# Layer 0 attention on Trainium2: scores in 64-row tiles with two heads side by side, linear attention in pieces at fixed places

## The chip, the core and the metric

The kernel runs on one core of one Trainium2 chip. A core has five engines with an instruction queue each: TensorE (PE in the profile, its weight loads PEld) multiplies matrices from SBUF into the accumulator memory PSUM, VectorE (DVE), ScalarE (ACT) and GpSimd (POOL) work element by element, and SyncE (SP) issues most DMAs. Each queue runs in its own order; an instruction that waits holds up all that stand behind it in the queue. The metric is the device time of one execution in microseconds, lower is better, shown as the median of several runs. The profile is one execution, with its span from the first to the last instruction.

## The reference

The model has two layers. Layer 0 runs two branches beside each other over 2304 tokens (256 context, 2048 latent); what is changed lies in these two, between their projections and the layer's output projection.

```python
def block_attention(q, k, v, scale):            # branch A: 8 heads of 64 + 32 = 96 dimensions
    ...
        s = jnp.einsum('bqhd,bkhd->bhqk', qi, k, preferred_element_type=jnp.float32) * scale
        p = jax.nn.softmax(s, axis=-1).astype(v.dtype)
        return jnp.einsum('bhqk,bkhd->bqhd', p, v)
...
def gla_scan(q, k, v, g, s0):                   # branch B: 4 heads, forward and backward, chunks of 64
    ...
    def step(state, inp):
        qi, ki, vi, gi = inp
        b = jnp.cumsum(gi, axis=-2)
        b_last = b[..., -1:, :]
        q_t = qi * jnp.exp(b)
        k_t = ki * jnp.exp(-b)
        att = jnp.where(mask, jnp.einsum('bhld,bhmd->bhlm', q_t, k_t), 0.0)
        o = jnp.einsum('bhld,bhde->bhle', q_t, state) + jnp.einsum('bhlm,bhme->bhle', att, vi)
        k_dec = ki * jnp.exp(b_last - b)
        state = state * jnp.exp(b_last)[..., 0, :, None] + jnp.einsum('bhld,bhle->bhde', k_dec, vi)
        return state, o
```

Of the 96 dimensions of a query and a key 64 are plain (`A_NOPE`) and 32 carry the rotary position (`A_ROPE`); a value has 64. Context queries attend to the 256 context keys, latent queries to all 2304. The gate logits of branch B come from 2 x 16 columns of the projection (`g_lr`); its result is normalised per head and gated before the output projection.

## The kernel before

**Attention (`even_attention`).** Everything is transposed: scores stand as [128 keys x up to 512 queries]. The outer loop goes over four head pairs `j`, the next over five query blocks (one of 256 context queries, four of 512 latent ones), the inner over key tiles of 128 keys: 18, or 2 for the context. For precision each operand of a score is split into two fp32r parts, high and low; of the four products three are taken: `kh` x `qh` (with a 97th row that carries a bias, L1097), `kh` x `ql` (L1098) and `kl` x `qh` (L1099), each over 96 or 97 rows of the array and 512 columns. They add up in one of three PSUM banks named `st`. ScalarE takes the exponential into SBUF (`apt`, L106, the helper through which all of ScalarE's operations go) and VectorE adds it to the running sum over keys (`acc`, L1088), head by head. Where six key tiles are pending, the value products of the four oldest are issued (`tail`, L1039): plain fp32, 64 columns of the array for each of the two heads, adding up in a bank `av`. `finish` then divides: two matmuls with a constant sum `acc` over keys (L970), and ScalarE's logarithm and exponential and VectorE's L975 to L977 make the quotient; it reads `av` directly, of which there are two banks.

**Linear attention (`gla`).** It goes over 18 chunks of 128 tokens in a first, a scanning and a second pass. `front` turns the gate columns round (L797), makes the logits (L803), the log-sigmoid (`ge`, `gG`) and its cumulated sums (L818, L819) and the factors `gqt`, `gkt`. `back` multiplies these with the inputs, turns them round (L847), makes the chunk's own state `D` (L852), the products within the chunk in 64-row tiles, backward and forward alternating (L861), and their output `goi` (L870). `scan` passes the states on: forward on GpSimd, backward on VectorE. `second` then adds the states' part (`enter`, L927 and L928), takes the sum of squares on VectorE, and in `leave` scales, gates and turns round (L945). All of it shares two PSUM banks `gl`.

**What sets the order.** The kernel is written against a framework that places each engine's instructions by its own estimate of when their inputs are ready; `issue_after` ties an instruction behind another one on its queue. Scores and value products are tied to each other, the pieces of the linear attention are not: the framework lays them between the score matmuls wherever they become ready. From key tile 174 on, `hook` gives out the second pass step by step (`next(slow)`), with the loads of the output projection's weights.

**Loads.** For each head pair, keys and their low parts come in thirds of 768 keys, one DMA for each, and queries in two DMAs per block, all issued by SyncE.

## Time and profile before

| | |
|---|---|
| median of 3 runs | 3543.79 us (3543.53 to 3548.53) |
| the profiled execution itself, its span | 3541.8 us |
| attention stretch of layer 0 | 1060 to 1902 us of the span |
| TensorE busy, whole span | 3477.8 us (98%) |
| VectorE, ScalarE, GpSimd busy, whole span | 2392.1, 1398.4, 1214.3 us |

The profiled execution lies 2.0 us below the median of the runs. In the groups of instructions, a row gives line, engine, operation, the tiles out<-in by the program's names, the shape and the count, then the busy time, the mean duration of one in ns, and the idle time of the engine ahead of them with what ended it. TensorE's instructions overlap, so their durations add up to more than the time they take. A plain fp32 matmul appears as two instructions and more on TensorE; the counts in the profile are of such instructions, those of the printed orders below of the program's.

### The profile page before, as it was taken

How to read it: one execution, taken by the hardware profiler on the slowest of the kernel's cores; microseconds unless marked ns; L12 is line 12 of the kernel's file. 1: busy time of each engine (PE TensorE's matmuls, PEld its weight loads, DVE VectorE, ACT ScalarE, POOL GpSimd, SP SyncE). 2: the span in 40 equal slices, each digit the busy share in tenths (PEclk: the TensorE clock that was granted, in tenths of full speed). 3: DMA queues.
4: the chain of work that ended last, by engine and by line, in shares of the span. 5: the costliest groups of instructions: out<-in, count | busy, mean ns of one | idle time of the engine just before them, and what ended most of it. 6: DMA issues, size and time to landing. Idle time of an engine off the chain costs nothing. (4 is left out here: it accounts for less than half of the span.)

```text
span 3541.8 us, 53493 instructions
## 1 busy us (share of the span) xinstructions
PE 3477.8 (98%) x19260; PEld 2752.4 (78%) x19260; DVE 2392.1 (68%) x5020; ACT 1398.4 (39%) x2656; POOL 1214.3 (34%) x1363
## 2 busy tenths in 40 slices
PE   8999999999999999999999999999999999999999
PEld 6998999999996666656667888888898987555587
DVE  4677767888886777788765345455598883777821
ACT  5555451111116555555553134444422223555510
POOL 1433330111111222211321233333354544777743
PEclk9999999999999999999999999999999999999999
DMA  6555564222243343434543554555844348878664
GB/s 246 161 148 169 149 196 116 78 76 85 68 124 83 80 111 85 101 84 115 161 119 126 169 174 124 143 161 156 255 152 146 123 128 224 217 210 218 187 184 149
DMA packets 386914, 513.75 MB, mean 145 GB/s; under 512 B 61229, under 2 KB 264061, under 8 KB 380746
## 3 DMA queue, kind: packets, MB, share of 16 engines
...
## 5 line engine op out<-in xcount | busy, mean ns | idle before, releaser
L1088 DVE TENSOR_TENSOR acc<-acc,apt 128x512 f32<-128x512 f32 x512 | 379.6, 772 | 142.2 <-ACT apt L106 139.5
L739 DVE TENSOR_REDUCE mm<-mx 128x1 f32<-128x512 f32 (+1 forms) x656 | 390.8, 628 | 87.8 <-PE mx L738 80.4
L106 ACT ACTIVATE apt<-st 128x512 f32<-128x512 f32 (+1 forms) x592 | 344.8, 594 | 247.3 <-PE st L1099 207.5
L1039 PE MATMUL av<-apt,av 128*64 128x512 f32 (+1 forms) x1184 | 270.0, 592 | 0.0
L1097 PE MATMUL st<-aq,akh 97*128 97x512 f32 x576 | 245.1, 426 | 1.0 <-ACT apt L106 1.0
L738 PE MATMUL mx<-mk,mq 96*128 96x512 f32 (+1 forms) x656 | 241.7, 371 | 0.0
L106 ACT ACTIVATE u<-gm 128x352 f32<-128x352 f32 (+1 forms) x144 | 70.8, 493 | 418.4 <-PE gm L131 182.6
L1098 PE MATMUL st<-aq,akh 96*128 96x512 f32 x576 | 228.2, 396 | 0.0
L1099 PE MATMUL st<-aq,akl 96*128 96x512 f32 x576 | 227.9, 396 | 0.0
L106 ACT ACTIVATE opt<-opt 128x930 f32<-128x930 f32 (+9 forms) x144 | 119.5, 831 | 254.5 <-POOL opt L1856 140.0
L1039 PEld LDWEIGHTS av<-apt,av 128*64 128x64 f32 x1184 | 80.1, 136 | 152.7 <-issue 149.7
L1554 DVE CUSTOM_DVE_ANT_1 mx<-mx,mtab 128x465 f32<-128x465 f32 (+12 forms) x576 | 180.3, 341 | 26.5 <-PE mx L1548 20.4
L1689 POOL TENSOR_TENSOR oacc<-oacc,opt 128x682 f32<-128x682 f32 (+9 forms) x144 | 170.3, 1200 | 40.6 <-ACT opt L106 39.1
L1818 DVE TENSOR_TENSOR opt<-st,tab 128x64 f32<-128x64 f32 (+10 forms) x576 | 142.3, 312 | 37.8 <-PE st L1654 33.2
L1097 PEld LDWEIGHTS st<-aq,akh 97*128 97x128 f32 x576 | 108.3, 188 | 72.6 <-issue 44.6
L1099 PEld LDWEIGHTS st<-aq,akl 96*128 96x128 f32 x576 | 109.5, 190 | 25.2
L738 PEld LDWEIGHTS mx<-mk,mq 96*128 96x128 f32 x656 | 123.3, 188 | 6.0
L1098 PEld LDWEIGHTS st<-aq,akh 96*128 96x128 f32 x576 | 109.9, 191 | 17.0
L106 ACT ACTIVATE x<-px,modB,modA 128x128 f32<-128x128 f32 x272 | 98.7, 465 | 55.9 <-PE px L362 32.5
L129 PE MATMUL gm<-w1h,hhi 128*128 128x512 f32 x288 | 115.1, 400 | 0.0
L1653 PE MATMUL st<-q,kt 128*128 128x480 f32 (+5 forms) x256 | 98.4, 386 | 16.8 <-DVE opt L1818 13.1
L131 PE MATMUL gm<-w0h,hlo 128*128 128x512 f32 x288 | 113.3, 393 | 1.5 <-DVE hlo L392 1.5
...
## 6 DMA issues: line engine op xcount, KB each, us to landing
...
```

Of the source, the lines that this page charges most:

```text
L106: return self.nc.scalar.activation(out, in_, func, **kw)
L129: self.nc.tensor.matmul(out, lh(k), rh(k), start=j == 0, stop=False)
L738: mm = nc.tensor.matmul(ps[:, :w], q[:A_QK, (t % 6) * P : (t % 6) * P + P], k[:A_QK, k0 : k0 + w], start=True, stop=True)
L739: nc.vector.tensor_reduce(out=m[:, t, n : n + 1], in_=ps[:, :w], axis=AX.X, op=ALU.max)
L1039: nc.tensor.matmul(O[j, nb][i * 64 : i * 64 + 64, :w], V[j, kt // TT][:, kt % TT, i * 64 : i * 64 + 64], pts[i][:, :w], start=n == 0, stop ...
L1088: self.add = nc.vector.tensor_tensor(out=acc[i][:, :w], in0=a[:, :w], in1=pts[i][:, :w], op=ALU.add)
L1097: nc.tensor.matmul(ps[:, :w], kh[: A_QK + 1, i, kq], qh[: A_QK + 1, :w], start=True, stop=False)
L1098: nc.tensor.matmul(ps[:, :w], kh[:A_QK, i, kq], ql[:A_QK, :w], start=False, stop=False)
L1099: mm = nc.tensor.matmul(ps[:, :w], kl[:A_QK, i, kq], qh[:A_QK, :w], start=False, stop=True)
L1554: nc.vector.tensor_tensor_reduce(out=s, in0=s, in1=tb[:, ri : ri + rn, ci : ci + cn], scale=1.0, scalar=-3e38, op0=ALU.add, op1=ALU.max, a ...
L1689: self.psum = nc.gpsimd.tensor_tensor(out=a, in0=a, in1=pts[:, :, a0 - r0 : a1 - r0, :], op=ALU.add)
L1818: badd = nc.vector.tensor_tensor(out=pt[:, d[0], d[1]], in0=ps[:, d[0], d[1]], in1=tabs[j][i][:, ri : ri + rn, ci : ci + cn], op=ALU.add)
```

## The change

**Scores.** `score` replaces the three products of each head by five of at most 64 rows: plain part high x high, high x low, low x high, then the rotary part's high and low keys (32 rows each, stacked) x high, and high x low with the bias row (33 rows). Head 0 of the pair lies on rows 0 to 63 of the array, head 1 on rows 64 to 127; the ten matmuls of a key tile alternate between them and are tied one behind the other. Keys, low parts and queries are laid out for it in SBUF: six DMAs for a third of the keys where there was one, two for the low parts, ten for a block of queries where there were two.

```diff
+        def score(j, kt, Q, ps, w):
+
+            kq = slice(kt % TT * P, kt % TT * P + P)
+            kh, kl = K[j, kt // TT], L[j, kt // TT]
+            mm = last_pe[0]
+            for k, kz, qz, n in ((kl, 0, 0, 64), (kl, 0, 1, 64), (kl, 1, 0, 64), (kh, 0, 2, 64), (kh, 1, 3, A_ROPE + 1)):
+                for i in range(2):
+                    r = slice(i * 64, i * 64 + n)
+                    with after(mm):
+                        mm = nc.tensor.matmul(ps[i], k[r, kz, kq], Q[r, qz, :w], start=qz == kz == 0 and k is kl, stop=k is kh and kz == 1)
+            last_pe[0] = mm
+            return mm
...
-                        ps = self.tl(pp, [P, 512], "st", bufs=3)
-                        nc.tensor.matmul(ps[:, :w], kh[: A_QK + 1, i, kq], qh[: A_QK + 1, :w], start=True, stop=False)
-                        nc.tensor.matmul(ps[:, :w], kh[:A_QK, i, kq], ql[:A_QK, :w], start=False, stop=False)
-                        mm = nc.tensor.matmul(ps[:, :w], kl[:A_QK, i, kq], qh[:A_QK, :w], start=False, stop=True)
-                        pt = self.tl(ap, [P, 512], "apt", bufs=14)
-                        ex = self.act(pt[:, :w], ps[:, :w], AF.Exp, scale=A_SCALE)
-                        pts.append(pt)
-                    add(n, pts)
+                    ps = [self.tl(pp, [P, 512], "st", bufs=4)[:, :w] for _ in range(2)]
+                    mm = score(j, kt, Q, ps, w)
+                    pt = self.tl(ap, [P, 2, 512], "apt", bufs=6)
                     for i in range(2):
+                        ex = self.act(pt[:, i, :w], ps[i], AF.Exp, scale=A_SCALE)
+                    if n == 0:
+                        first = pt
+                    else:
+                        self.add = nc.vector.tensor_tensor(out=acc[:, :, :w], in0=(first if n == 1 else acc)[:, :, :w], in1=pt[:, :, :w], op=ALU.add)
...
             for a, b in parts(j, p):
-                nc.sync.dma_start(kh[:A_QK, :, a:b].bitcast(F32),
-                                  self.KT[2 * j : 2 * j + 2, 0, :A_QK, p * W + a : p * W + b].rearrange("h p t -> p h t"))
+                for i in range(2):
+                    r, src = i * 64, self.KT[2 * j + i, :, A_NOPE:A_QK, p * W + a : p * W + b]
+                    for u, z in ((0, 0), (0, 1), (1, 0)):
+                        nc.sync.dma_start(kh[r + z * A_ROPE : r + z * A_ROPE + A_ROPE, u, a:b].bitcast(F32), src[z])
```

On TensorE one key tile of 512 queries reads as follows; `st` are the score banks, `aq` the queries, `akh` and `akl` the keys' tiles. Before:

```order
L1097 MATMUL st_12898<-aq_12816,akh_1772_10749 128x512
L1098 MATMUL st_12898<-aq_12816,akh_1772_10749 128x512
L1099 MATMUL st_12898<-aq_12816,akl_10761 128x512
L1097 MATMUL st_12904<-aq_12816,akh_1772_10749 128x512
L1098 MATMUL st_12904<-aq_12816,akh_1772_10749 128x512
L1099 MATMUL st_12904<-aq_12816,akl_10761 128x512
```

and with the change:

```order
L1216 MATMUL st_11689<-aq_11367,akl_10809 128x512
L1216 MATMUL st_11690<-aq_11367,akl_10809 128x512
L1216 MATMUL st_11689<-aq_11367,akl_10809 128x512
L1216 MATMUL st_11690<-aq_11367,akl_10809 128x512
L1216 MATMUL st_11689<-aq_11367,akl_10809 128x512
L1216 MATMUL st_11690<-aq_11367,akl_10809 128x512
L1216 MATMUL st_11689<-aq_11367,akh_1773_10750 128x512
L1216 MATMUL st_11690<-aq_11367,akh_1773_10750 128x512
L1216 MATMUL st_11689<-aq_11367,akh_1773_10750 128x512
L1216 MATMUL st_11690<-aq_11367,akh_1773_10750 128x512
```

Six steps, one head after the other, became ten, of which each two neighbours belong to different heads; the first bank is complete with the ninth instead of the third.

**PSUM, sums and the quotient.** There are four `st` banks, so that two key tiles of two heads fit, three `gl` banks, and one `av` bank; the bank `den` goes. VectorE adds both heads of a key tile in one instruction, 1024 wide. Where a block's value products end, ScalarE copies `av` to SBUF (`take`); the matmuls with the constant follow ahead of the next group of value products (`divide`), and VectorE's part (`newton`) behind that group's last key tile.

```diff
+        def flush():
+
+            dens, room = list(taken), 3 - len(taken)
+            taken.clear()
+            for x in dens:
+                run(ending, *x)
+            for x in [pend.pop(0) for _ in range(min(4, len(pend)))]:
+                if x[2] == 0 and taken and room:
+                    hook(room, run)
+                    room = 0
+                run(tail, *x)
+            if room:
+                hook(room, run)
...
+                    behind(ex, *([self.add] if n else []))
+                    if len(pend) == 6:
+                        flush()
+                    elif len(pend) == 4:
+                        hook(0, run)
```

**Linear attention.** `front` and `back` are cut into pieces, each with one TensorE part: `ranks` (three chunks at once, L812), `logits` (L823), `middle` (L842, L843), `turn` (L871), `local` (L881), `within` (L894), `inner` (L909); the second pass into `join` (L997) and `leave` (L1022). `run` ties each behind TensorE's last matmul, so that none stands between the scores of a key tile. A planner gives them out: behind each group of four value products as many as there are free `gl` banks (three), each piece only if what it reads was made a group earlier (`fwd`, `may`); halfway through the next four key tiles `hook(0)` issues the elementwise multiplications that `turn` reads (`times`) and one `within`. After the forward pass `enter` places one `leave` and one `join` behind each group; halfway run `scale` and `more`, which loads the output projection's weights one by one.

```diff
+        def may(what, c):
+
+            t = now[0]
+            if what == ranks:
+                return c % 3 == 0 and had(logits, c - 4)
+            return {logits: lambda: had(ranks, c - c % 3, t) and had(middle, c - 1),
+                    middle: lambda: had(logits, c, t) and had(turn, c - 1) and had(local, c - 1) and had(inner, c - 2),
+                    turn: lambda: had(middle, c, t) and had(within, c - 1),
+                    local: lambda: had(middle, c, t),
+                    within: lambda: had(turn, c) and had(inner, c - 1),
+                    inner: lambda: had(within, c, t) and had(local, c)}[what]()
...
+            for what in (inner, turn, local, middle, logits, ranks):
+                for c in range(NT):
+                    n = 2 if what == turn else 1
+                    if (what, c) not in done and n <= room and may(what, c):
+                        room -= n
+                        done[what, c] = now[0]
+                        picked.append((order.index(what), what, c))
```

Value products and what follows them read on TensorE as follows; `av` is their bank, `gl` a bank of the linear attention. Before:

```order
L1039 MATMUL av_12926<-apt_12874,av_10763 64x512
L1039 MATMUL av_12926<-apt_12880,av_10763 64x512
L1097 MATMUL st_12935<-aq_12816,akh_1773_10750 128x512
L1098 MATMUL st_12935<-aq_12816,akh_1773_10750 128x512
L1099 MATMUL st_12935<-aq_12816,akl_10772 128x512
L818 MATMUL gl_10917<-gG_10880,trr_10789 128x4x64
L819 MATMUL gl_10917<-ge_10882,trr_10789 128x4x64
L818 MATMUL gl_10917<-gG_10880,trr_10789 128x4x64
L819 MATMUL gl_10917<-ge_10882,trr_10789 128x4x64
L861 MATMUL gl_10932<-gqT_10890,gkT_10891 128x128
```

and with the change:

```order
L1166 MATMUL av_11543<-apt_11579,av_10812 64x512 x2
L1166 MATMUL av_11543<-apt_11600,av_10812 64x512 x2
L881 MATMUL gl_11659<-gu_10892,gkt_11432 128x128 x4
L842 MATMUL gl_11665<-gG_11447,trr_10833 128x4x64
L843 MATMUL gl_11665<-ge_11440,trr_10833 128x4x64
L842 MATMUL gl_11665<-gG_11447,trr_10833 128x4x64
L843 MATMUL gl_11665<-ge_11440,trr_10833 128x4x64
L823 MATMUL gl_11677<-gw_10827,rT_1792_10841 128x512
L1216 MATMUL st_11689<-aq_11367,akl_10809 128x512
```

The linear attention moved from between the scores to one place behind the value products, here with three pieces (`local`, `middle`, `logits`).

**Which engine does what.** The backward scan goes from VectorE to GpSimd, the copy of `D` and the sums of squares from VectorE to ScalarE:

```diff
-            nc.vector.tensor_copy(Dl[c][:].rearrange("p h t -> p (h t)"), ps[:])
+            self.act(Dl[c][:].rearrange("p h t -> p (h t)"), ps[:])
...
-        scan(list(range(NT)), slice(0, 64), nc.gpsimd, "gsf")
-        scan(self.back_order(), slice(64, 128), nc.vector, "gsb")
...
+                g.tensor_tensor(out=N[sl], in0=S[sl], in1=f[sl, 3, :].unsqueeze(2).to_broadcast([64, H, P]), op=ALU.mult)
+                g.tensor_tensor(out=N[sl], in0=N[sl], in1=d[sl], op=ALU.add)
+                g.tensor_tensor(out=d[sl], in0=S[sl], in1=f[sl, 1, :].unsqueeze(2).to_broadcast([64, H, P]), op=ALU.mult)
...
-                nc.vector.tensor_tensor_reduce(out=sq[:, o], in0=oi[:, o], in1=oi[:, o], scale=1.0, scalar=0.0,
-                                               op0=ALU.mult, op1=ALU.add, accum_out=ss[:, h : h + 1])
+                self.act(sq[:, each[h]], oi[:, each[h]], AF.Square, accum_out=ss[:, h : h + 1])
```

ScalarE's queue at the burst of scores that follows the rows above; every row is the helper L106, `apt` out of `st` is an exponential of scores. Before, around a comparable chunk:

```order
L106 ACTIVATE ge_11030<-gl_11028 128x512
L106 ACTIVATE apt_13138<-st_13134 128x512
L106 ACTIVATE ge_11030<-ge_11030 128x512
L106 ACTIVATE apt_13144<-st_13140 128x512
L106 ACTIVATE ge_11030<-ge_11030 128x512
L106 ACTIVATE apt_13150<-st_13146 128x512
L106 ACTIVATE goi_11045<-gl_11040 128x512
```

and with the change:

```order
L106 ACTIVATE D_1796_10851<-gl_11659 128x512
L106 ACTIVATE gqt_11670<-gl_11665 128x512
L106 ACTIVATE gkt_11671<-gl_11665 128x512
L106 ACTIVATE gt_11680<-gl_11677 128x512
L106 ACTIVATE gt_11680<-gt_11680 128x512
L106 ACTIVATE apt_11701<-st_11689 128x512
L106 ACTIVATE gt_11680<-gt_11680 128x512
L106 ACTIVATE apt_11701<-st_11690 128x512
L106 ACTIVATE apt_11717<-st_11705 128x512
L106 ACTIVATE apt_11717<-st_11706 128x512
L106 ACTIVATE gG_11686<-gt_11680 128x512
```

Where one instruction of the linear attention stood between two exponentials, five now stand ahead of the burst's first exponential and one between its two.

393 lines of the change are left out of this document (231 added, 162 removed).

## The prediction

> **What bounds the kernel now.** I read the page's first and fifth part, then layer 0's attention alone in the windows view, then what TensorE waits for there, then its timeline for the cadence. Ahead of the change's stretch and behind it nothing is edited, so those parts of the span are kept as they are.
>
> ```profile
> span 3541.8 us, 53493 instructions
> ...
> PE 3477.8 (98%) x19260; PEld 2752.4 (78%) x19260; DVE 2392.1 (68%) x5020; ACT 1398.4 (39%) x2656; POOL 1214.3 (34%) x1363
> ...
> L1097 PE MATMUL st<-aq,akh 97*128 97x512 f32 x576 | 245.1, 426 | 1.0 <-ACT apt L106 1.0
> ```
> ```profile
> 1060.00:1902.00 842.00, 836.17 (x4119) 521.39 (x4120) 628.13 (x1027) 482.03 (x926) 185.26 (x187) 1.00 0.38 101
> ```
> ```profile
> PE st L1097 <- ACT apt L106: 2.2, 3, 1.2
> PE gl L870 <- DVE gat L866: 1.8, 5, 0.6
> PE den L970 <- DVE rc L976: 1.4, 1, 1.4
> PE gl L803 <- DVE ge L864: 0.2, 1, 0.2
> ```
> The second fence is the attention stretch, 1060 to 1902 (behind the length: busy us and count of PE, PEld, DVE, ACT, POOL; granted clock; DMA share; GB/s), the third all waits of TensorE in it. The stretch is TensorE's: busy 836 of 842 us at the full granted clock (1.00), with only 5.6 us of waits, while VectorE (628), ScalarE (482) and GpSimd (185) have room. So a shorter instruction list on TensorE shortens the kernel, until another engine ends the wait. What one step costs there stands in the timeline:
>
> ```profile
> 1116.01 1.05 PE L852 MATMUL gl<-gu,gkt 128*128 128x128 f32 x8
> 1116.89 0.27 PE L797 MATMUL gl<-ident,gu 128*96 128x128 f32 x1
> ...
> 1118.18 0.40 PE L1099 MATMUL st<-aq,akl 96*128 96x512 f32 x1
> 1118.51 1.08 PE L970 MATMUL den<-acc,mtwos 128*64 128x512 f32 x4
> 1119.41 3.60 PE L1039 MATMUL av<-apt,av 128*64 128x512 f32 x16
> 1122.95 0.50 PE L1097 MATMUL st<-aq,akh 97*128 97x512 f32 x1
> 1123.29 0.40 PE L1098 MATMUL st<-aq,akh 96*128 96x512 f32 x1
> ...
> 1125.08 0.40 PE L1098 MATMUL st<-aq,akh 96*128 96x512 f32 x1
> ...
> 1126.72 0.40 PE L1099 MATMUL st<-aq,akl 96*128 96x512 f32 x1
> 1127.05 1.16 PE L861 MATMUL gl<-gqT,gkT 64*128 64x128 f32 x14
> 1128.13 0.50 PE L1097 MATMUL st<-aq,akh 97*128 97x512 f32 x1
> ```
> Durations overlap here, so I go by starts. Seven score steps lie between 1125.08 and 1126.72: 0.234 us each.
>
> **The scores: the gain.** Before, a key tile takes 2 heads x 3 products = 6 steps, 1.405 us; there are 576/2 = 288 such pairs 512 wide and 8 pairs 256 wide. After, it takes 10 matmuls of 64 rows, the two heads alternating on rows 0 to 63 and 64 to 127. If the two run side by side that is 5 steps, 1.17 us, and the gain is 288 x 0.234 + 8 x 0.12 = 68.4 us. Whether they do: L861 of the linear attention is already such an alternation. Its 14 instructions take 1128.13 - 1127.05 = 1.08 us; less 0.2 us for changing the array's form (below), that is 0.126 per pair, while one full-height L852 of the same width takes (1116.89 - 1116.01)/8 = 0.110. Two for the price of nearly one. But L861 is plain fp32, and the trace has no fp32r instruction of 64 rows. Bounds: quickest, a step costs what one pass of the value products does (16 instructions in 3.44 us without the form change, two heads side by side, two passes each: 0.215), which gives 288 x 5 x 0.019 = 27 us more; slowest, no overlap, 10 x 0.234 = 2.34 us, a loss of 269 us. I take 0.234: the tile's shape is L861's, the operand's rate is L1098's.
>
> The Trainium skill (TensorE: Matmul & The Clock Gate, Measured speedup vs the span model) lets packed tiles take one matmul's duration plus about 4 ns for each further tile. By it each step would be 4 ns dearer, an estimate of 288 x 5 x 0.004 = 5.8 us, and the sum below would end 6 us higher; no row here settles so small a term.
>
> **The fixed order: form changes.** Entering another form (full height, half height, half width) costs 1118.51 - 1118.18 - 0.234 = 0.10 us, and the first matmul in it lasts 1123.29 - 1122.95 = 0.34 instead of 0.234, another 0.11. Counted along TensorE's order between the first score and the last value product, there are 222 changes before and 221 after: scores now always differ in form from what surrounds them, but the linear attention no longer stands among them except for `within`, which has their form. I cost it at nothing. Its matmuls are as many as before (18 chunks of each piece).
>
> **Waits that go.** The pieces that waited for VectorE (L870, L970, L803: 3.4 us) now stand one group behind what they read: -3.4 us. Of L1097's 2.2 us, the longest (1.2) is at the first exponential; I leave all of it.
>
> **Waits that come: ScalarE.** Before, three score banks went round one by one, an exponential every 0.70 us of TensorE time, and linear-attention work was spread between them. After, the four banks are two pairs, and ScalarE's queue holds a whole group's linear-attention instructions ahead of the first exponential of the next four key tiles.
>
> ```profile
> 1414.22 1.30 ACT L106 ACTIVATE apt<-st 128x512 f32<-128x512 f32 x2
> ...
> 1414.49 0.40 PE L1099 MATMUL st<-aq,akl 96*128 96x512 f32 x1
> ```
> ```profile
> 1102.51 0.60 ACT L106 ACTIVATE gqt<-gl 128x512 f32<-128x512 f32 x1
> 1102.99 0.62 ACT L106 ACTIVATE gkt<-gl 128x512 f32<-128x512 f32 x1
> 1103.46 0.65 ACT L106 ACTIVATE ge<-ge 128x512 f32<-128x512 f32 x1
> 1103.98 1.60 ACT L106 ACTIVATE apt<-st 128x512 f32<-128x512 f32 x3
> ```
> ```profile
> 1103.93 0.40 PE L1099 MATMUL st<-aq,akl 96*128 96x512 f32 x1
> 1104.66 0.50 PE L1097 MATMUL st<-aq,akh 97*128 97x512 f32 x1 [0.34 <-ACT apt L106]
> ```
> An exponential starts 0.43 us behind its tile's last step (1414.22 + 1.30 - 0.60 = 1414.92, against 1414.49). Back to back, ScalarE starts one each 0.48 us (0.52 where it reads SBUF); one lasts 0.60, and TensorE follows 0.05 later. The last fence is the mechanism at work already: `gqt`, `gkt` and `ge` of the linear attention stood ahead of the exponentials, and TensorE came 0.50 us late (0.73 between the starts instead of 0.234).
>
> The walk of one burst of four key tiles, from its first step: pair 1's last step starts at 1.04, its exponentials run 1.47 to 2.07 and 1.95 to 2.55, and pair 3, due at 2.44, needs the second bank: **0.17 us late**, then the two heads run staggered and lose no more. Behind the waiting matmul stand, in TensorE's fixed order, the rest of the burst and the value products, so each such wait is lost in full. Where five instructions stand ahead (`local`, `middle`, `logits`: the first begins 0.6 before the burst, as its product is done) and a sixth between the two exponentials, the second exponential ends at 3.44: **1.05 late**. With `middle` or `logits` beside another piece, four to five ahead: **0.6**. In the second pass:
>
> ```profile
> L106 ACT ACTIVATE gsb<-gl,gn 128x128 f32<-128x128 f32 x72 | 20.4, 373 | 1.9 <-PE gl L945 1.8
> ...
> L106 ACT ACTIVATION_READ_ACCUMULATOR sql<-u 128x1 f32 x72 | 13.7, 190 | 0.0
> ...
> L928 DVE TENSOR_TENSOR goi<-gl,goi 128x512 f32<-128x512 f32 x18 | 12.4, 691 | 1.7 <-PE gl L927 1.5
> ```
> `join`'s four squares, moved from VectorE, wait for the 0.69 us add, start at about 0.9, and cost between 20.4/72 = 0.28 each and 0.28 + 0.19; I take 0.33, nearer the first, since neighbours overlap. The second exponential then ends at 3.3: **0.9 late**. By the printed order there are 8 bursts of the heavy kind, 10 of the middling, 17 with `join`, 18 that `within` cuts in two (its 1 us gives ScalarE time: 0), and 21 others: 8 x 1.05 + 10 x 0.6 + 17 x 0.9 + 21 x 0.17 = 33 us. From below, 56 x 0.17 = 9.5; from above, 1.1 in all 74, 81 us.
>
> **What I cost at nothing, and its cover.** GpSimd gets the backward scan:
>
> ```profile
> L907 POOL TENSOR_TENSOR gsf<-gsf,D 64x512 f32<-64x512 f32 x17 | 27.1, 1593 | 1.3
> L222 POOL TENSOR_TENSOR gss<-gss,mhalf 128x4 f32<-128x4 f32 x18 | 23.1, 1285 | 1.5
> L942 POOL TENSOR_TENSOR goi<-goi,gsf 128x512 f32<-128x512 f32 x18 | 22.9, 1272 | 34.6 <-issue 25.7 <-DVE goi L941 5.6 <-PE av L1039 1.7
> L908 POOL TENSOR_TENSOR D<-gsf,fac 64x512 f32<-64x512 f32 x17 | 22.7, 1335 | 1.3
> L906 POOL TENSOR_TENSOR gsf<-gsf,fac 64x512 f32<-64x512 f32 x17 | 22.3, 1311 | 1.3
> ...
> L220 POOL TENSOR_SCALAR gss<-gss 128x4 f32<-128x4 f32 x18 | 9.6, 533 | 93.7 <-DVE gss L933 93.7
> ```
> One group of the second pass asks 1.31 + 1.59 + 1.34 + 1.27 + 0.53 + 1.29 = 7.3 us of it, in a group of some 9.9 (four pairs 4.7, value products 3.5, `leave` and `join` 1.5, form changes), and the scan runs one chunk ahead. Each us beyond would delay 17 joins. VectorE only loses work; its joined adds hold up nobody nearer than six key tiles on. SyncE issues about 120 more loads; at 0.4 us that is 48 us of its time, ahead of use by a block, except at the start:
>
> ```profile
> 1015.87 0.32 SPq L1026 DMA_DIRECT2D aqc<-QT  x1
> ...
> 1035.92 0.85 SPq L1015 DMA_DIRECT2D av<-Vn  x1
> ```
> ```profile
> 1058.67 0.36 PE L1097 MATMUL st<-aqc,akh 97*128 97x256 f32 x1
> ```
> The 22 extra issues ahead of the second block take some 11 us of the 22 between the last load's issue and the first score. Behind the stretch the same work follows.
>
> **The sum.** 3541.8 - 68.4 - 3.4 + 33 = 3503 for the profiled execution; the runs' median, 3543.8, lies 2.0 above its span, so **3505 us**, 39 us (1.1%) faster.
>
> **The rivals.** (A) *The halves don't run side by side in fp32r.* For: no row of this form. Against: L861. It decides from a step of (1.405 + 0.012)/5 = 0.283 us, since ScalarE then waits for TensorE and the 33 us vanish; without any overlap, 3543.8 + 269 - 3.4 = 3809. Slower, 0.09 from 0.283 up. (B) *ScalarE paces most bursts*, as a chain: late exponentials, late logits, late pieces. For: 1104.66 above; against: it has 3.5 us of value products in every group to catch up, and two exponentials (0.96) fit in a pair (1.17). Every burst 1.1 late: 3541.8 - 68.4 - 3.4 + 81 + 2 = 3553; from half of that on, 3530 to 3556, chance 0.12. The Trainium skill has it as a rule (TensorEngine Tiling (Array Packing), PSUM Bottleneck): tiling speeds the products up but not the emptying of PSUM, which may become the bound; by the rows it cannot be so in the mean, only in the burst. (C) *ScalarE keeps up*: only the 0.17s stay, 3541.8 - 68.4 - 3.4 + 9.5 + 2 = 3481; for it, bursts are followed by 3.5 us of value products; against it, the printed order of its queue. 0.24. (D) *Steps at 0.215*: 27 us less, 3478; 0.08. (E) *The order or the loads undo it* (a late load, a piece that waits on GpSimd): no change, 3543; 0.02.
>
> **How the numbers follow.** The forecast has 0.45, on its own range 3485 to 3530. What a measurement of this kernel can tell from no change is about 0.2%, 7 us. Faster: 0.45 + 0.24 + 0.08 and half of B, 0.83; within 0.2%: the rest of B below 3551, and E, 0.06; slower: A and the end of B, 0.11. The range 3470 to 3545 leaves out A, the upper half of B and a part of D: about 0.17.
>
> **What would show it.** Right: steps of two score matmuls start 0.23 to 0.24 us apart, the two within 0.02; TensorE's waits in the stretch come to 20 to 45 us, nearly all of scores on `apt`, in bursts behind `logits` and `join`; about as many form changes; the stretch is some 39 us shorter and the rest alike. Wrong: a step of 0.28 or more (A); waits of 60 us or more on `apt` (B), or under 15 (C); pieces that wait for GpSimd's `D`, or scores for `akh` and `aq` (E).

## The result: 1.2% slower

The changed kernel takes 3587.73 us (median of four runs, 3584.38 to 3588.99), the kernel before beside it 3543.66 us: a ratio of 1.012 with an interval of 1.0106 to 1.0134. The forecast was 3505 us. The profiled execution of the changed kernel took 3588.85 us, its span opens the page:

```profile
span 3587.0 us, 55633 instructions
...
PE 3461.6 (97%) x20444; PEld 2717.1 (76%) x20444; DVE 2300.1 (64%) x4529; ACT 1417.0 (40%) x2838; POOL 1301.6 (36%) x1424
```

TensorE is busy 16.2 us less than before (3477.8), and the span is 45.2 us longer. The attention stretch, from the first score to the last value product, in the windows view (behind the length: busy us and count of PE, PEld, DVE, ACT, POOL, granted clock, DMA share, GB/s), of the kernel before:

```profile
1058.70:1893.20 834.50, 828.66 (x4092) 515.97 (x4093) 626.05 (x1024) 480.19 (x923) 183.87 (x186) 1.00 0.39 101
```

and of the changed one:

```profile
1063.90:1942.30 878.40, 811.20 (x5275) 479.42 (x5277) 541.61 (x532) 497.06 (x1103) 268.80 (x243) 0.96 0.39 101
```

The stretch is 44 us longer and starts 5.2 us later (3.8 of that comes up ahead of any edited code, about 3.0 of it at a wait of 2.5 us for VectorE near 545 us with half speed behind it; 1.3 is a wait for the projection's `u` ahead of the first score); what follows it is 4 us shorter. So the loss lies in the stretch. Three things changed in it. TensorE stood idle for 67.2 us (878.4 less 811.2) instead of 5.8. Its granted clock fell to 0.96: by the clock record ten windows of together 71.7 us ran at half speed, where before there was none, and half of TensorE's busy time in them is 26.4 us. What is left, its own work at full speed, is 811.2 - 26.4 = 784.8 instead of 828.7. Work -44, half speed +26, idle +61. TensorE's waits there:

```profile
PE st L1216 <- ACT apt L106: 36.0, 33, 6.1
PE gl L1022 <- POOL goi L1012: 18.2, 3, 8.1
PE gl L812 <- DMA gu<-Un: 7.8, 2, 5.1
PE av L1166 <- ACT oy L106: 2.1, 2, 1.4
```

**The steps are as forecast.** An undisturbed stretch of the timeline, two key tiles and `within`:

```profile
1287.79 0.86 PE L1216 MATMUL st<-aq,akl 64*128 64x512 f32 x6
1288.48 0.62 PE L1216 MATMUL st<-aq,akh 64*128 64x512 f32 x4
1288.94 1.05 PE L894 MATMUL gl<-gqT,gkT 64*128 64x128 f32 x16
```

The ten matmuls of the key tile take 1288.94 - 1287.79 = 1.15 us, five steps of 0.230 (forecast 0.234), and the two of a step start 3 to 4 ns apart. Over the stretch the bursts of two key tiles run at 1.23 us a tile with the form change in it (median, less idle time and half speed). The bursts of four run at 1.39, where (4 x 1.15 + 0.2)/4 gives 1.20. Part of that belongs to every burst of four, as one shows for which ScalarE has nothing but exponentials to do:

```profile
1888.56 0.96 PE L1216 MATMUL st<-aq,akl 64*128 64x512 f32 x6
1889.82 0.86 PE L1216 MATMUL st<-aq,akl 64*128 64x512 f32 x6
1890.98 0.90 PE L1216 MATMUL st<-aq,akl 64*128 64x512 f32 x5
1891.72 0.39 PE L1216 MATMUL st<-aq,akh 64*128 64x512 f32 x1
1891.72 0.39 PE L1216 MATMUL st<-aq,akl 64*128 64x512 f32 x1
...
1893.68 0.65 PE L1166 MATMUL av<-apt,av 128*64 128x512 f32 x2
```

It takes 1893.68 - 1888.56 = 5.12 us, 0.3 more than 4.8. From the third tile on one head runs a step behind the other (at 1891.72 `akh` of one starts beside `akl` of the other), and the fourth tile takes 1.49 us, since its last step runs alone. In 53 bursts of four that is 16 us; those that take clearly more are the ones that wait besides. In all, score bursts took 442.9 us before and 440.1 after, with the idle time and the half speed inside them; the steps' gain was used up there.

**The heavy burst is as forecast too.** In one place of the timeline, ScalarE and TensorE:

```profile
1104.48 0.60 ACT L106 ACTIVATE gqt<-gl 128x512 f32<-128x512 f32 x1 [3.38 <-PE gl L843]
...
1105.45 0.61 ACT L106 ACTIVATE gt<-gl 128x512 f32<-128x512 f32 x1
...
1105.89 0.86 PE L1216 MATMUL st<-aq,akl 64*128 64x512 f32 x6
...
1106.63 0.58 ACT L106 ACTIVATE apt<-st 128x512 f32<-128x512 f32 x1
1107.10 0.62 ACT L106 ACTIVATE gt<-gt 128x512 f32<-128x512 f32 x1
...
1107.26 0.49 PE L1216 MATMUL st<-aq,akl 64*128 64x512 f32 x1
...
1107.62 1.56 ACT L106 ACTIVATE apt<-st 128x512 f32<-128x512 f32 x3
...
1108.27 0.96 PE L1216 MATMUL st<-aq,akl 64*128 64x512 f32 x5 [0.51 <-ACT apt L106]
...
1109.30 1.07 PE L1216 MATMUL st<-aq,akl 64*128 64x512 f32 x6
```

Four instructions of the linear attention stand ahead of the first exponential, a fifth between it and the second. The third key tile, due 1.15 us behind the second's 1105.89, begins with one matmul alone at 1107.26; the other head's bank comes free only behind the second exponential, and five matmuls follow at 1108.27. The fourth tile starts at 1109.30 instead of 1105.89 + 2 x 1.15 = 1108.19: 1.11 us late, where the walk had 1.05. Only 0.51 of it stands as idle time in front of a row; during most of the rest one half of the array worked alone and counts as busy. So the view of waits understates what a late exponential costs here.

**The longest wait is of another kind.** At 1500 us, SyncE's queue (SPq), ScalarE, VectorE and TensorE:

```profile
1494.40 2.09 SPq L1143 DMA_DIRECT2D aq<-QT  x2
...
1496.09 0.59 ACT L106 ACTIVATE gqt<-gl 128x512 f32<-128x512 f32 x1
...
1498.05 3.79 SPq L1113 DMA_DIRECT2D akh<-KT  x6
...
1499.23 0.59 ACT L106 ACTIVATE apt<-st 128x512 f32<-128x512 f32 x1
...
1503.24 0.52 SPq L848 DMA_DIRECT2D gE<-gqt  x2
...
1504.94 0.69 DVE L861 TENSOR_TENSOR gqt<-gqt,gu 128x512 f32<-128x512 f32 x1 [10.82 <-DMA gE<-gqt]
1505.55 0.68 DVE L829 SCALAR_TENSOR_TENSOR gt<-gl,gt 128x512 f32<-128x512 f32 x1
...
1506.26 0.63 ACT L106 ACTIVATE gG<-gt 128x512 fp32r<-128x512 f32 x1 [6.45 <-DVE gt L829]
1506.80 1.07 ACT L106 ACTIVATE apt<-st 128x512 f32<-128x512 f32 x2
...
1507.43 2.13 PE L1216 MATMUL st<-aq,akl 64*128 64x512 f32 x6 [6.14 <-ACT apt L106]
```

Four queues hand the delay on. SyncE issues the next head pair's queries and keys until 1503.2. Behind them stands the store of two rows of `gqt` (L848, issued at 1503.24), which ScalarE had finished at 1496.68. VectorE's multiplication L861 writes `gqt` in place, so it has to wait for that store, 10.8 us. Behind it on VectorE stands L829, which makes `gt`; for `gt` ScalarE's `gG` waits, and behind `gG` stands the exponential that TensorE needs. Then the matmuls come slowly: the windows view of the wait and of what follows it,

```profile
1500.00:1507.00 7.00, 1.29 (x9) 0.73 (x9) 1.97 (x4) 0.74 (x2) 0.00 (x0) 0.84 0.34 94
1507.00:1511.00 4.00, 3.57 (x12) 2.07 (x14) 1.96 (x3) 2.19 (x6) 0.89 (x3) 0.50 0.43 56
```

has a granted clock of 0.50 behind it. VectorE's waits for that store grew from this, before,

```profile
DVE gqt L840 <- DMA gE<-gqt: 6.8, 3, 4.1
```

to this:

```profile
DVE gqt L861 <- DMA gE<-gqt: 40.4, 10, 10.8
```

**The third kind is GpSimd.** Timeline at 1610 us, of the backward scan (L929 to L931) and the second pass:

```profile
1609.90 1.04 POOL L931 TENSOR_TENSOR D<-gsb,fac 64x512 f32<-64x512 f32 x1
...
1618.19 1.04 POOL L929 TENSOR_TENSOR gsb<-gsb,fac 64x512 f32<-64x512 f32 x1
1619.32 0.20 POOL L220 TENSOR_SCALAR gss<-gss 128x4 f32<-128x4 f32 x1
...
1622.02 0.69 DVE L1011 TENSOR_TENSOR goi<-goi,gss 128x512 f32<-128x512 f32 x1 [12.73 <-POOL gss L222]
...
1623.69 2.12 POOL L1012 TENSOR_TENSOR goi<-goi,gsf 128x512 f32<-128x512 f32 x1
...
1625.86 1.11 PE L1022 MATMUL gl<-ident,goi 128*128 128x128 f32 x4 [5.71 <-POOL goi L1012]
```

From 1589 to 1619 GpSimd works without a pause on eight scan steps (six of them whole), and `leave`'s power (L220, L222) and gating (L1012) of the current chunk stand behind them; VectorE waits 12.7 us, TensorE 5.7, and 4.4 and 8.1 more at the next two `leave`s.

Sorted by what ended them, the delays are: 57 us of late scores (idle, and half of the array alone, beyond the 5.12 us of an undisturbed burst of four), of which 18 fall while ScalarE worked on its own queue and 39 while ScalarE itself stood waiting for VectorE or a DMA; 19 at `leave`; 8 at the first `ranks`, whose rows had not landed; 26 of half speed. This is worked out from the start times, step by step, and is an estimate; the runs below test its larger terms.

### The profile page after: what moved, and what is told of

Its sections match the earlier page's. It is cut to its first block, busy times and chain, and to the rows that moved or that the text cites. A ratio compares the mean times of both kernels' runs of the same rounds, so it can differ in the third digit from the quotient of the medians.

```text
span 3587.0 us, 55633 instructions
## 1 busy us (share of the span) xinstructions
PE 3461.6 (97%) x20444; PEld 2717.1 (76%) x20444; DVE 2300.1 (64%) x4529; ACT 1417.0 (40%) x2838; POOL 1301.6 (36%) x1424
## 4 chain that ended last, share of the span: by engine, by line
PE 52%; POOL 3%; ACT 2%; DVE 2%; DMA 2%; issue 2%; SPq 0%; POOLq 0%; ACTq 0%; DVEq 0%
PE gm L131 5%; PE gm L129 5%; PE gm L130 5%; PE st L1216 5%; PE av L1166 4%; PE st L1809 2%; PE o L1839 2%; PE st L129 2%; PE st L131 2%; PE st L130 2%; PE st L1810 2%; PE pj L131 2%; PE o L1821 2%; PE pj L129 2%; PE pj L130 2%
## 5 line engine op out<-in xcount | busy, mean ns | idle before, releaser
L1253 DVE TENSOR_TENSOR acc<-acc,apt 128x1024 f32<-128x1024 f32 x256 | 361.3, 1411 | 157.5 <-ACT apt L106 145.7
L106 ACT ACTIVATE apt<-st 128x512 f32<-128x512 f32 (+1 forms) x592 | 312.4, 590 | 93.9 <-PE st L1216 86.2
L1216 PE MATMUL st<-aq,akl 64*128 64x512 f32 x1728 | 307.2, 420 | 37.7 <-ACT apt L106 36.0
L1216 PEld LDWEIGHTS st<-aq,akl 64*128 64x128 f32 x1728 | 176.0, 190 | 122.9 <-ACT apt L106 76.1
L106 ACT ACTIVATE u<-gm 128x352 f32<-128x352 f32 (+1 forms) x144 | 70.7, 493 | 417.9 <-PE gm L131 182.6
L106 ACT ACTIVATE opt<-opt 128x930 f32<-128x930 f32 (+9 forms) x144 | 119.5, 831 | 253.9 <-POOL opt L2012 140.3
L1216 PE MATMUL st<-aq,akh 64*128 64x512 f32 (+1 forms) x1152 | 211.6, 397 | 0.0
L1710 DVE CUSTOM_DVE_ANT_1 mx<-mx,mtab 128x465 f32<-128x465 f32 (+12 forms) x576 | 180.9, 342 | 27.2 <-PE mx L1704 20.9
L1974 DVE TENSOR_TENSOR opt<-st,tab 128x64 f32<-128x64 f32 (+10 forms) x576 | 143.0, 319 | 43.5 <-PE st L1810 40.4
L1216 PEld LDWEIGHTS st<-aq,akh 33*128 33x128 f32 (+1 forms) x1152 | 133.4, 189 | 25.6
L106 ACT ACTIVATE x<-px,modB,modA 128x128 f32<-128x128 f32 x272 | 98.7, 465 | 54.9 <-PE px L362 38.6
L129 PE MATMUL gm<-w0h,hhi 128*128 128x512 f32 x288 | 114.2, 397 | 0.0
L222 POOL TENSOR_TENSOR oss<-oss,mhalf 128x8 f32<-128x8 f32 x68 | 112.2, 1650 | 5.5
L130 PE MATMUL gm<-w1l,hhi 128*128 128x512 f32 x288 | 114.2, 397 | 0.0
```

Source lines behind the costliest of these rows:

```text
L106: return self.nc.scalar.activation(out, in_, func, **kw)
L129: self.nc.tensor.matmul(out, lh(k), rh(k), start=j == 0, stop=False)
L130: self.nc.tensor.matmul(out, lh(k), rl(k), start=False, stop=False)
L1216: mm = nc.tensor.matmul(ps[i], k[r, kz, kq], Q[r, qz, :w], start=qz == kz == 0 and k is kl, stop=k is kh and kz == 1)
L1253: self.add = nc.vector.tensor_tensor(out=acc[:, :, :w], in0=(first if n == 1 else acc)[:, :, :w], in1=pt[:, :, :w], op=ALU.add)
L1710: nc.vector.tensor_tensor_reduce(out=s, in0=s, in1=tb[:, ri : ri + rn, ci : ci + cn], scale=1.0, scalar=-3e38, op0=ALU.add, op1=ALU.max, a ...
```

## The experiments

The theory was that three handed-on delays, (1) GpSimd's scan, (2) SyncE's late stores and loads through VectorE and ScalarE, and (3) ScalarE's own queue, eat a gain of the tiles that is real. Against it stood: the tiles themselves don't pay; the number of loads is the cause; the order of the pieces alone is. For each run the stretch of its profiled execution is split as above. The kernel before, measured beside each, lay between 3542.4 and 3545.1 us, so the ratios compare better than the times do:

| | median us | ratio to before | stretch | idle | half speed | work |
|---|---|---|---|---|---|---|
| before | 3543.66 | | 834.5 | 5.8 | 0 | 828.7 |
| the change | 3587.73 | 1.0120 | 878.5 | 67.2 | 26.4 | 784.9 |
| scan on VectorE | 3571.49 | 1.0082 | 859.5 | 55.3 | 19.2 | 784.9 |
| scan tied on GpSimd | 3561.82 | 1.0052 | 851.1 | 48.1 | 17.1 | 785.9 |
| order with 96-row scores | 3578.42 | 1.0098 | 869.0 | 39.5 | 13.7 | 815.7 |
| the same, loads split | 3566.87 | 1.0061 | 858.1 | 31.1 | 11.3 | 815.7 |
| 64-row scores alone | 3653.87 | 1.0312 | 947.4 | 88.0 | 71.0 | 788.4 |
| all three relieved | 3549.12 | 1.0012 | 841.1 | 51.6 | 8.2 | 781.4 |
| the same, 96-row scores | 3566.98 | 1.0065 | 860.6 | 37.3 | 7.0 | 816.4 |
| relieved, scan tied | 3543.44 | 1.0006 | 833.5 | 42.7 | 10.4 | 780.4 |

**GpSimd's scan.** First the backward scan went back to VectorE (`eng` below), nothing else.

```diff
+            eng = g if name == "gsf" else nc.vector
-                g.tensor_tensor(out=N[sl], in0=S[sl], in1=f[sl, 3, :].unsqueeze(2).to_broadcast([64, H, P]), op=ALU.mult)
+                eng.tensor_tensor(out=N[sl], in0=S[sl], in1=f[sl, 3, :].unsqueeze(2).to_broadcast([64, H, P]), op=ALU.mult)
```

> The changed kernel with the backward scan on VectorE again; nothing else differs. In its profile TensorE waits 18.2 us, 3 times, at the first leaves (L1022) for GpSimd's goi, which stands behind scan steps that the framework laid ahead of it, and the clock record shows half speed for some us behind each. Theory GpSimd: these three waits go, with some 5 us of half-speed work behind them: 3587.7 - 24 = 3564 us, no wait on goi over 1 us. Theory SyncE (the leaves are late because their loads are) or no slack anywhere: the waits stay or move to another piece, 3580 to 3592 us. VectorE's added work (3 steps of some 0.7 us a chunk, 36 us in all) would show as longer waits of scores on apt, by at most 5 us.

3571.49 us, ratio 1.0082 (1.0065 to 1.0099), 16 us faster than the change. The waits for `goi` are gone; those on `apt` grew from 36.0 to 43.3 us. Whether GpSimd is too slow or only goes in the wrong order, a later run tells: the scan stays on GpSimd, but each step is tied behind the gating L1012 of its group.

```diff
-                g.tensor_tensor(out=oi[:], in0=oi[:], in1=zb, op=ALU.mult)
+                done["scaled"] = g.tensor_tensor(out=oi[:], in0=oi[:], in1=zb, op=ALU.mult)
-                scan(scans.pop(0), back, "gsb")
+                with self.tc.issue_after(done["scaled"].ins) if "scaled" in done else ExitStack():
+                    scan(scans.pop(0), back, "gsb")
```

> The changed kernel, the backward scan still on GpSimd, with one tie: each scan step behind the same group's multiplication of goi. Theory lump: the three waits on goi (18.2 us) go with their half speed, as they did with the scan on VectorE: 3560 to 3572 us. Theory GpSimd too slow: the waits move to the joins, which need D from the step before: one of a few us for each of 17 joins, 3600 us or more.

3561.82 us, 1.0052 (1.0038 to 1.0065): 26 us faster than the change by one tie. TensorE's waits in it have no row for GpSimd:

```profile
PE st L1217 <- ACT apt L106: 35.5, 31, 6.3
PE gl L812 <- DMA gu<-Un: 7.1, 2, 4.4
```

So GpSimd is fast enough; the framework, for which the scan steps were ready early, had laid them in a lump ahead of the second pass. The stretch is 27.4 us shorter: 19.1 of idle time and 9.3 of half speed less, 1.0 of work more. A wait cost about half as much again here as it shows.

**The tiles against the order.** The change's order with the 96-row scores and their few loads of before:

```diff
-            for k, kz, qz, n in ((kl, 0, 0, 64), (kl, 0, 1, 64), (kl, 1, 0, 64), (kh, 0, 2, 64), (kh, 1, 3, A_ROPE + 1)):
-                for i in range(2):
+            for i in range(2):
+                for k, qz, n in ((kh, 2 * i, A_QK + 1), (kh, 2 * i + 1, A_QK), (kl, 2 * i, A_QK)):
```

> The changed kernel with the scores as before: three products of 96 or 97 rows for each head, one head after the other, and the old loads; everything else (pieces at fixed places, engines, banks) as changed. If a key tile's tiled scores are worth 0.234 us as their steps of 0.23 us say, TensorE has 68 us more work: 3587.7 + 68 = 3656 us with the waits as they are. Theory SyncE and ScalarE: with the old loads and slower steps the waits on apt fall by half or more, 30 to 45 us with the half speed behind them: 3610 to 3625 us, still well over before's 3543.8, since the waits for GpSimd (19) and for the first rows (8) and the half speed behind these stay. Theory that the tiled form itself costs (weight loads, form changes): under 3590 us.

3578.42 us, 1.0098 (1.0083 to 1.0113): 9 us *faster* than with the tiles, though TensorE has 31 us more work. The reverse, the kernel before with the tiled scores, their loads, four score banks and the quotient's matmuls in `gl`, and the linear attention scheduled as before:

> The kernel before with the scores alone changed: tiles of 64 rows, two heads side by side, their loads, four score banks, the divisor's matmul in a bank of the linear attention; the linear attention stays as it was and is placed by the framework. Its printed order has 264 changes of the array's form against 222. If the steps alone count: 3543.8 - 68.4 + 42 x 0.2 = 3484 us. Theory SyncE (the extra loads do the harm): 3484 + 28 = 3510 us or more, with late transfers. Theory fixed order (the harm is the fixed places without slack): 3480 to 3495 us, waits of TensorE in the stretch under 15 us. If the tiled form itself is at fault: 3540 us or more.

3653.87 us, 1.0312 (1.0297 to 1.0327), 110 us slower. Its waits of TensorE are those of the linear attention's pieces, not of scores:

```profile
PE gl L803 <- DVE ge L864: 26.2, 15, 4.9
PE gl L870 <- DVE gat L866: 21.0, 18, 4.3
```

and VectorE waits 44.2 us for the store of `gqt`. With those stores, and the load of `fac` that reads them, on GpSimd's queue (`nc.gpsimd.dma_start` instead of `nc.sync.dma_start` at four lines) it takes 3630.93 us, 1.0251 (1.0237 to 1.0265):

> The kernel before with tiled scores alone (3654 us: 88 us idle, 71 us lost at half speed), its boundary rows (gE, fac) stored and loaded by GpSimd instead of SyncE. There VectorE waited 44 us, 16 times, for the store of gqt's rows before it could multiply in place. Theory SyncE's order (those stores stand behind query and key loads, the pieces placed between scores then stop TensorE): most of the idle time goes and with it the half speed: 3490 to 3540 us. Theory pace (at the tiled rate the chain of a piece through ScalarE and VectorE is too slow for its place in any case): 3600 us or more.

SyncE's place in that chain thus accounts for 23 of the 110 us; the waits for `gat` are still 29.5 us. Why the pieces come so late there I have not settled. Neither part of the change pays by itself.

**The number of loads.** Three runs: the change with merged loads (six DMAs for a third of the keys to three, ten for the queries to eight); the 96-row run above with its loads split into as many DMAs as the change has; the change with few loads of the old shape, which leaves out the layout by which each score gets its right rows.

```diff
+                src = self.KT[2 * j : 2 * j + 2, :, A_NOPE:A_QK, p * W + a : p * W + b]
+                nc.sync.dma_start(kh[:, 0, a:b].bitcast(F32), src)
-                        nc.sync.dma_start(kh[r + z * A_ROPE : r + z * A_ROPE + A_ROPE, u, a:b].bitcast(F32), src[z])
+                    nc.sync.dma_start(kh[i * 64 : i * 64 + A_ROPE, 1, a:b].bitcast(F32), src[i, 0])
```

> The changed kernel with the same layout but fewer load instructions: three DMAs instead of six for a third of the keys, eight instead of ten for a block of queries, about 80 fewer on SyncE's queue. Theory SyncE: the extra loads make the stores and loads behind them late, and ScalarE's in-order queue passes that on to the exponentials: of the waits on apt those of 6.3 (behind logits), 2.2 and 5.5 us (behind the projection's weights) and the fac ones shrink, some 18 us, and some 10 us of half-speed work behind them go: about 3560 us. Theory no slack (these transfers are as late anyway, since each is asked for only one group ahead): 3580 to 3592 us, the same waits.

> The kernel with 96-row scores of the run before (3578 us, 2.0 us of waits on apt), its loads cut into as many instructions as the tiled layout needs: six for a third of the keys, two for their low parts, ten for a block of queries. Theory SyncE (the number of loads on its queue makes the transfers behind them late): waits on apt of 10 us and more come back, with half speed behind them, 3590 to 3605 us. Theory pace (the tiled scores are fast enough to run into everything that is late; the loads are innocent): 3574 to 3583 us, waits on apt under 5 us.

> The changed kernel, matmul for matmul, but loaded with two DMAs for a third of the keys, two for the low parts and two for a block of queries, in rows of 96 and 32 as they stand in memory: the scores then multiply the wrong rows (and low key parts in place of high ones), so they are left out as a result while every instruction on TensorE, ScalarE, VectorE and GpSimd stays. Theory SyncE: the long waits on apt that hang on late transfers (6.3 us behind logits, 2.2 and 5.5 behind the projection's weights, the fac ones) go, with the half speed behind them: 3587.7 - 18 - 12 = 3558 us or less. Theory pace: those waits stay, 3580 to 3592 us.

The merged loads made it 62 us worse: 3650.17 us, 1.0301 (1.0285 to 1.0316). While a burst of loads holds everything up in that run, its windows view shows

```profile
1545.00:1550.00 5.00, 0.00 (x0) 0.00 (x0) 0.00 (x0) 0.00 (x0) 0.00 (x0) 0.50 0.26 82
1550.00:1555.00 5.00, 0.00 (x0) 0.00 (x0) 1.47 (x3) 0.14 (x1) 0.00 (x0) 0.50 0.14 40
```

where such a burst in the changed kernel had

```profile
1490.00:1495.00 5.00, 4.96 (x30) 2.31 (x31) 3.98 (x6) 1.67 (x5) 0.00 (x0) 1.00 1.01 289
```

TensorE stands still, and the others nearly so, at 40 to 82 GB/s instead of 289. The merged DMAs begin with a dimension of two (the heads or parts). The Trainium skill (DMA: Bandwidth & Descriptors, Why a DMA increments its semaphore by 16 and not by 1) has a DMA spread over the largest number of engines, up to 16, that divides the slowest dimension on both sides, here two, which would be a share of 2/16 = 0.125; the measured 0.14 lies near it, and 0.26 near twice that, far from 1.01. The split loads were not slower but 12 us faster, 3566.87 us, 1.0061 (1.0043 to 1.0079), and the few old-shaped ones 11 us slower, 3599.11 us, 1.0158 (1.014 to 1.0175). With these last the waits on scores did fall, from 36.0 to 27.2 us, but those for the first rows rose from 7.8 to 18.0. More loads are not the cause, and fewer no cure. The split run also has the change's number of loads with 96-row scores; its waits on scores are

```profile
PE st L1212 <- ACT apt L106: 4.4, 5, 2.9
```

against 36.0 with the tiles: same pieces, same places, as many loads. Less is late there, however: VectorE waits 9.9 us for the store of `gqt` instead of 40.4. With few loads and 96-row scores it waits 27.5 us for it, and TensorE only 2.0 on scores. So less lateness and more time until it reaches TensorE can both be behind the difference; no run separates them.

**SyncE unblocked, ScalarE relieved.** From the run with the scan on VectorE, step by step. First, loads and stores that wait on SyncE (the quotient's store, the gate's load, the output weights) went to GpSimd's queue; to it was added, in one run, a start of the linear attention two groups later; in another, `join`'s squares and the copy of `D` back on VectorE; then, on top of the latter, the weights' high part on VectorE and the small stores and loads of `gE` and `fac` on GpSimd's queue.

```diff
-                    nc.sync.dma_start(self.RT[j, :, q0 : q0 + w], rc)
+                    nc.gpsimd.dma_start(self.RT[j, :, q0 : q0 + w], rc)
```

> The changed kernel with the backward scan on VectorE (3571 us) and three kinds of transfers issued by GpSimd instead of SyncE: the store of the attention's result, on which SyncE waits 166 us in the stretch, the load of the gate into a tile that GpSimd has read (96 us of waits), and the load of the projection's weights. Theory SyncE, blocked rather than busy: transfers behind these come earlier, the waits on apt behind logits and weights go: 3540 to 3555 us. Theory pace: 3565 to 3575 us. Theory GpSimd is now too slow with some 0.55 us for each transfer: waits on goi come back, over 3575 us.

> The kernel before this one, with the linear attention's first pieces given out two groups later. The first piece waits for its rows from memory in every kernel of the fixed order (7.9 us in the changed kernel, half speed for 10 us behind it). Theory fixed places: that wait and its half speed go, 8 + 4 = 12 us less than the run before, and nothing is added, since the forward pass ends long before the attention does. If the rows are late for another reason: the same time as the run before.

> The kernel with SyncE unblocked (3561 us; TensorE idle for 53 us of the stretch, 16 us lost at half speed), and what the change gave to ScalarE back on VectorE: the copy of D and the sums of squares. Theory ScalarE (its linear-attention pieces ahead of the exponentials cost the time): of that run's waits those behind the squares (six of 1.4 to 2.1 us, two of 5.7 and 7.0 us that also have a late add in them) and the hidden ones in the heavy bursts go: 15 to 25 us less, 3536 to 3546 us. Theory late transfers (ScalarE waits in its order for loads and stores, not for its own work): the waits behind the squares move to VectorE's queue, and the time stays within 6 us, 3555 to 3566 us.

> The run before, with the last two kinds of transfers that ScalarE's order hangs on taken out of it: the projection's weights are split by VectorE alone, so that no ScalarE instruction waits for their load, and the boundary rows of the linear attention (gE, fac) are stored and loaded by GpSimd. Theory late transfers: of the 40 us of waits on apt 12 us behind weights and logits go, with their half speed, 15 to 20 us less than the run before; with the theory ScalarE both right, 3520 to 3530 us, 0.4% to 0.7% faster than the kernel before. Theory pace (any lateness stops TensorE at this rate, only its place changes): 3535 to 3560 us.

They took 3560.91 us (1.0053, 1.0036 to 1.0071), 3561.07 (1.0048, 1.0033 to 1.0063), 3552.0 (1.0025, 1.0013 to 1.0036) and 3549.12 (1.0012, 1.0003 to 1.0021). Idle time on `apt` went 43.3, 40.2 (33.3 with the later start, which moved the wait: `av` on `oy` rose to 6.6), 28.7 and 9.1. The times of neighbouring steps differ by little, and their intervals overlap or nearly do; the waits are clearer. Delays by ScalarE's own instructions and by late transfers are thus both likely; the last step moved two things at once, so no run separates their shares. But with each, other waits came up: of `leave` on `goi`, first none, then 10.7, then 27.8 us.

The last of these with 96-row scores again:

> The run before with 96-row scores and their loads. It tells what the tiles are worth once the rest no longer stops TensorE: by their steps 68 us. Theory pace: most of that is given back in waits, since 96-row scores leave ScalarE 1 us more for each bank: 3540 to 3550 us here, less than 30 us over the tiled version. Theory late transfers and ScalarE, both now mended: 3580 to 3600 us, 60 us or more over it.

3566.98 us, 1.0065 (1.0053 to 1.0078): 18 us slower than with the tiles, where before the relief the 96-row scores with the same few loads were 9 us faster. The tiles pay as soon as ScalarE is in time. How much is open: this run has the few loads, whose first rows come late (13.1 us of waits against 7.6), and splitting them was worth 12 us before the relief; split loads were not tried here.

**What is left.** On the relieved kernel, the scan steps of VectorE were tied behind the scaling of their group, and the weights' load went back to SyncE:

```diff
+                done["scaled"] = nc.vector.tensor_tensor(out=o3, in0=o3, in1=ss[:].unsqueeze(2).to_broadcast([P, H, P]), op=ALU.mult)
-                scan(scans.pop(0), back, "gsb")
+                with self.tc.issue_after(done["scaled"].ins) if "scaled" in done else ExitStack():
+                    scan(scans.pop(0), back, "gsb")
```

> The run in which all transfers were mended (3549 us) with two edits: each step of the backward scan is tied behind the same group's scaling on VectorE, so that the framework cannot lay several steps in a lump ahead of a join's add, and the projection's weights are loaded by SyncE again, since their load held GpSimd up for 11.8 and 6.8 us. There TensorE still waited 27.8 us in three leaves for goi, whose chain began with a join's add behind a lump of scan steps on VectorE. Theory lump (the scan steps were given out ahead of what is needed first): those waits go with their half speed, 30 us less: 3515 to 3525 us, 0.6% to 0.8% faster than the kernel before. Theory VectorE full (it has no room for scan, squares, splits and sums there): waits on goi of 15 us or more stay, 3535 to 3555 us.

3543.44 us, ratio 1.0006 (0.9997 to 1.0015): as fast as before, no faster. Its waits:

```profile
PE gl L1025 <- POOL goi L1014: 23.3, 10, 4.0
PE st L1219 <- ACT apt L106: 5.9, 14, 0.7
```

48 us less of work stand against 37 of idle time and 10 of half speed more. Nor do the tiles save what their steps promise: the relieved kernels with 64 and with 96 rows differ by 35 us of work (781.4 against 816.4), not by 68. Bursts of four run at 1.28 us a tile there (median), the 1.28 of the undisturbed burst above. With the scan tied on GpSimd behind the power and the gating multiplication on VectorE, 3543.2 us, 1.0001 (0.9992 to 1.0009), the `leave`s wait 25.1 us, now for VectorE:

> The tied kernel (3543 us; 42 us idle, 23 of it in nine leaves that wait 1 to 3 us for goi; VectorE busy for 176 of the 200 us from 1600) with two moves in the second pass: the scan goes to GpSimd again, each step tied behind the same group's power, and the gating multiplication of goi goes to VectorE, where it takes 0.7 us for GpSimd's 1.3 to 2.1. Theory engines balanced badly (VectorE too full, GpSimd's step late): the waits on goi fall to under 8 us, with some half speed: 3523 to 3533 us, 0.3% to 0.5% faster than the kernel before. Theory chain too long for its place (join, sum, power, scaling, gating and leave in one group of some 10 us, whatever the engines): 15 us and more of waits on goi, 3538 to 3548 us.

Whichever engine does the last multiplication, add, squares, power, scaling and gating don't end within the group that the fixed order gives them. A version with `leave` a group later was not tried.

Loading the first rows and inputs ahead of the constants gave nothing, 3546.86 us, 1.0012 (1.0003 to 1.0021); the first pieces then waited 9.8 us:

> The first kernel of this call with the linear attention's first rows and inputs loaded ahead of its constants, where they stood behind them. TensorE waits 7.6 us for those rows at the first piece, in half speed for some 10 us behind it. Theory SyncE's order: 3 to 8 us of the wait go, and some of the half speed, 4 to 10 us less than the first kernel of this call. Theory space (the tile is free only when the stretch before has ended): the same within 3 us.

**Half speed.** To see whether idle time itself causes it, 28 constant matmuls with no reader were put ahead of the first `ranks`, and, since that wait is at the second one (8.2 us) and the half-speed window stayed, ahead of both (11 and 26):

```diff
+            for _ in range({0: 11, 3: 26}.get(c0, 0)):
+                nc.tensor.matmul(ps[:, each[0]], self.ident[:], self.ident[:], start=True, stop=True)
```

> The other kernel of this call with 28 matmuls of a constant, 6.2 us by the 0.22 us that a full-height one of this width takes, into the first piece's bank ahead of it, where TensorE waits 5 to 8 us for the rows; their results are overwritten. Theory idle time brings the half speed: the half-speed window that stands behind this wait in every kernel of the fixed order (10 us at 1070 to 1076) is gone from the record, and the stretch is 3 to 5 us shorter. Theory the load or the power of the work brings it: the window stays, and the time is the same or 1 to 2 us longer.

> The filled kernel with the filling where its profile shows the waits: 11 matmuls of a constant (2.6 us) ahead of the first piece and 26 (6 us) ahead of the second, whose rows are asked for only when the first has been read and come 6 to 8 us later. Beside the unfilled kernel (3543 us, half speed for 10.2 us from 1069). Theory idle time brings the half speed: no half-speed window between 1060 and 1090, and the time is 1 to 5 us shorter, though the filling itself saves nothing. Theory that the half speed answers to the load: the window stays.

Windows without them (the run with the scan tied behind the power),

```profile
1070.00:1080.00 10.00, 4.25 (x15) 1.29 (x13) 2.38 (x7) 1.64 (x6) 0.00 (x0) 0.53 0.76 163
```

and with both:

```profile
1070.00:1080.00 10.00, 8.18 (x72) 7.85 (x71) 2.16 (x5) 2.09 (x6) 0.25 (x1) 1.00 0.75 204
```

The granted clock is 1.00 instead of 0.53: work that nobody needs kept TensorE at full speed there. The time gained nothing by it, 3549.61 us, 1.002 (1.0011 to 1.0029), and 3548.46, 1.0012 (1.0003 to 1.0021). With both, idle time in the stretch fell from 44.5 to 37.9 us, but work rose from 781.5 to 790.9, and as much of the stretch ran at half speed as without them (23.9 us), at other places.

## Why the prediction was wrong

In us of the stretch, the prediction's terms against what the trace has:

| term | forecast | measured |
|---|---|---|
| steps of the scores | -68.4 | -73: 288 x (1.405 - 1.15) |
| waits of before | -3.4 | -3.4 |
| scores late behind ScalarE's own work | +33 | +18 |
| scores late while ScalarE itself waits | 0 | +39 |
| `leave` behind GpSimd | 0 | +19 |
| first rows | 0 | +8 |
| half speed | 0 | +26 |
| every burst of four, one head a step behind | 0.17 a burst, within the 33 | +16 |
| rest: three small waits 4.6, not attributed -10 | 0 | -5.4 |
| sum | -39 | +44 |

**Right**: two heads run side by side in fp32r (rival A falls), at a step slightly under the 0.234 taken; rival D's 0.215 did not come. The walk of the heavy burst held, 1.11 us late for 1.05. ScalarE's own term held in sum, 18 + 16 = 34 us for 33, in part by luck: the undisturbed burst loses 0.3 us where the walk had 0.17 and "lose no more", as the head that is a step behind ends alone. Rival B, ScalarE pacing the bursts, had the right place (scores on `apt`) and the wrong cause: 39 of the 57 us are not ScalarE's work, and in the relieved kernel `apt` costs 9.1 us of idle time. The bound of 60 us on `apt` as B's sign was not reached either, in the view of waits: 36.0, with more hidden in staggered halves.

**Wrong, first:** "the scan runs one chunk ahead", and with it 7.3 us of GpSimd in a group of 9.9. The load was right, the order was not. I counted the work of a group and did not look at where the scan's rows stand in GpSimd's queue; there eight steps precede the first L220. The tied run shows 26 us for it, half speed included.

**Wrong, second:** "SyncE issues about 120 more loads ... ahead of use by a block". They are 238 more, 305 instead of 67, and take 112 us of SyncE's time instead of the 48. Ahead of *their own* use they are. But the stores of `gE`, which share the queue, now stand behind them, and VectorE's in-place multiplication stands behind the stores, ScalarE's `gG` behind VectorE, an exponential behind `gG`. The prediction named queues one by one, not the chain through four of them. In the kernel before the same chain existed (6.8 us of waits for the store), but a score bank of the 96-row kind is full, and its exponential issued, with more time in hand: in the split-loads run the same order costs 4.4 us on `apt`, with less waiting for the store (9.9 us). That the time in hand is what absorbs it is my reading; shown is only the difference of 4.4 to 36.0. Nor is it shown that the number of loads makes the stores late: with few loads of the old shape VectorE waits 44.8 us for them. That such chains held the scores up is shown by their relief: with these stores on GpSimd's queue and the weights split on VectorE the waits on `apt` fell from 28.7 to 9.1 us, though others took their place.

**Wrong, third:** nothing in the sum allowed for the clock. The attention stretch ran at 1.00 before, but the trace had a price elsewhere, in the windows view around a long wait of the output projection:

```profile
2535.00:2565.00 30.00, 23.61 (x142) 20.95 (x140) 11.55 (x12) 4.41 (x7) 12.66 (x8) 0.94 0.61 209
```

6% of 30 us, 1.8 us, went there to the clock behind one wait. Ten such places would make 18 of the 26.

Rival E ("the order or the loads undo it") was nearest, at no change and a chance of 0.02; most of the new waits are of its kind, only larger. I had set its chance by the few waits in the kernel before, which say nothing on an order that did not exist there.
